# Moving the attention values' products two score tiles behind their pair's second turn

## The chip, the cores and the metric

The kernel runs on one NeuronCore of a Trainium2 chip. The metric is the device time of one execution in microseconds (us). Two kernels are compared by runs on the same chip; the kernel before was run three times.

## What is computed

One layer of a hybrid encoder block on 512 tokens of width 2048, in float32: an adaLN-modulated RMS norm, one input projection, two token mixers that read the projected columns, a gate on each, one output projection, a gated residual and a last RMS norm. The part that matters here is the first mixer, attention with 16 heads of 64 columns. A query sees keys in three dilated windows; their outputs are merged with weights from the softmax denominators. Cut to its core, the reference says:

```python
for window, dilation in ((128, 1), (512, 4), (2048, 16)):
    o_p, lse_p = dilated_window_attention(aq, ak, av, rel_bias, window, dilation)
mix_w = jax.nn.softmax(jnp.stack(lses, axis=0), axis=0)
att = jnp.einsum('pbsh,pbshe->bshe', mix_w, jnp.stack(outs, axis=0))
```

The kernel folds the three patterns into one softmax: a key that several windows see gets the logarithm of its multiplicity, one that none sees gets a huge negative bias. So each head has one score matrix, one exponential, one normalisation and one product with the values.

## The kernel before

**Units.** TensorE is the engine whose order is written out by hand: `tc.manual_schedule(engines={E.PE})` makes its program order the order of the code. On the other engines (ScalarE, here ACT; VectorE, here DVE; GpSimd, here POOL; and SP, which issues most DMAs) the framework orders the instructions by priority and by what is ready. The large products are cut into units; `unit(name, ...)` computes 512 columns of the input projection in four PSUM chains. A unit has 8 groups of weights (two tiles of 128 input rows each), and in a group every chain gets two calls of `three` (L227 to L230): a product in high and low halves, three matmuls of 512 columns. Each call is a **tick**, so a unit has 64 ticks. The units `qk2`, `qk4`, `qk6` and `gk` follow one another, and each carries the attention of four heads as side work: a list of pairs (share of the unit, function). A function is called, and its TensorE instructions are thus placed, after the first tick that is not below its share times 64. What has a share of 1 or more goes into `spill` and comes at the head of the next unit.

**The attention items.** `attention(pairs)` cuts four heads into 16 score tiles (4 per head, `h`, `i`), numbered here 0 to 15, and has three kinds of items for them.

- `score(h, i)`, L819 and L820: two matmuls (128 queries, 416 keys) into a PSUM tile `s`; DVE adds the bias and takes the extreme (L827, two pieces), ACT takes the exponential with its sum (L831), DVE the reciprocal (L834), POOL scales the tile `p` (L842; for the last two tiles of head 15 ACT does, L840). An odd tile is scaled in two pieces, one of which goes into free columns of the even tile's buffer. The second tile of a head also issues the DMA of the next head's bias (L806, on SP's queue).
- `turn(h, i)`, L857: three transposes of `p` into a PSUM tile `t`; ACT copies its high half (L861) and DVE subtracts for the low half (L862), both into the buffer `pt`. The turn of an odd tile calls `rest` (L870): a fourth transpose, into a tile `r` of the PSUM ring `pj`, of the columns that the pair shares, then two small copies on ACT (L875) and two small subtractions on DVE (L877).
- `values(h, e)`, L886: for a pair of tiles eight matmuls of 256 columns into a PSUM tile `o`, over four chunks of keys and the high and low halves of `pt`, chunk 0 last; ACT copies half of the result (L889) and DVE adds it to the other half (L893).

`pt` exists twice, one for each pair of a head, and the next head writes the same two again. `s`, `t` and `o` share the PSUM ring `pa` with three buffers, so each of these items takes the buffer of the third one before it. The ring `pj` has five: four for the unit's chains and one for `r`.

**Their order.** The list of items is built by a loop over `x`: score tile `x`, then the turn of tile `x - 2`, then, where that tile is odd, the values of the pair that ends with tile `x - 3`. The 40 items are spread evenly over the unit, from share 0.17 on, 0.02 apart; the first two are moved a little ahead, and the last one, the values of pair 14/15, is moved behind the unit's end, to the first tick of the next.

**Around it.** While the heads of one unit are worked on, the unit computes the queries and keys of later heads. After its last tick `qk_evict` (L757 on) moves them out of PSUM: for each head two ACT copies (L766, L773) and two DVE operations (L767, L775), with DMAs to make the other half's copies. The chains of the next unit need these PSUM buffers. After `gk` four ACT copies (L1265) do it. Beside the scores DVE also splits weights (L476, behind ACT's L492) and does sums that other stages need.

Of the kernel before, what the change touches and what calls it, by code (L numbers as in the profile page):

```python
# [189 lines left out]
def block_kernel(ctx: ExitStack, tc: tile.TileContext, a: dict):  # L190
# [485 lines left out]
    n = len(chain) // 2  # L676
# [121 lines left out]
    def attention(pairs):  # L798
# [47 lines left out]
        def turn(h, i):  # L846
            def go():
                e, half = divmod(i, 2)
                if len(pts) == e:
                    pts.append(B8(f"pt{e}", [2, 4, 256], F32R))  # L850
                    nc.gpsimd.memset(pts[e][:, :, 3, 0:P].bitcast(F32), 0.0)
                    nc.gpsimd.memset(pts[e][:, :, 0, P:2 * P].bitcast(F32), 0.0)
                pt, t = pts[e], pr_[h, i]
                pk = PA(f"t{h}{i}")
                first_ = 0 if half else 128
                for kt in range(3):
                    nc.tensor.transpose(pk[:, kt * P:kt * P + P], t[:, first_ + kt * P:first_ + kt * P + P], ident)  # L857
                hi = pt[:, 0, half:half + 3, P * half:P * half + P]
                lo = pt[:, 1, half:half + 3, P * half:P * half + P]
                src = pk[:, :3 * P].rearrange("p (k q) -> p k q", k=3)  # L860
                act(hi, src, AF.Copy)  # L861
                tt(lo, src, hi.bitcast(F32), op=ALU.subtract)  # L862
                if half:
                    rest(h, e)
            return go
# [13 lines left out]
        def values(h, e):  # L879
            def go():  # L880
                t = pts[e]
                po = PA(f"o{h}{e}")
                order = (1, 2, 3, 0)
                for n_, c in enumerate(order):
                    for w in range(2):
                        mm(po[:, :256], vv[h // 4][:, CHUNK_OF[e][c], h % 4, :], t[:, w, c, :],  # L886
                           start=n_ == 0 and w == 0, stop=n_ == 3 and w == 1)
                oh = sm.tile([64, 256], F32, tag="oh", name=f"oh{h}{e}", bufs=1)
                act(oh, po[64:128, :256], AF.Copy)  # L889
                own = stacks[h][3]  # L890
                p = h // 2
                dst = cat[p // 4][own, p % 4, :].rearrange("p (c e) -> p e c", e=2)[:, 1 - e, :]
                tt(dst[:, ::-1], po[0:64, :256], oh, op=ALU.add)  # L893
            return go

        items = []
        n = len(tiles)
        for x in range(n + 3):
            if x < n:
                items.append(score(*tiles[x]))  # L900
            if 2 <= x <= n + 1:
                items.append(turn(*tiles[x - 2]))
            v = x - 3
            if 0 <= v < n and tiles[v][1] % 2 == 1:
                items.append(values(tiles[v][0], tiles[v][1] // 2))
        g_load(heads[0])
# [348 lines left out]
    for n, p in (("qk2", 0), ("qk4", 2), ("qk6", 4)):  # L1255
        ps = unit(n, False, attention((p, p + 1)) + ([(0.05, shift_row)] if p == 2 else []))
        for q in range(2):
            qk_evict(p + 2 + q, ps[2 * q], ps[2 * q + 1])

    ps = unit("gk", False, attention((6, 7)))  # L1260
    kp_.close()
    gs = mid.enter_context(tc.tile_pool(name="gs", bufs=1, reuse_waits="tile"))
# [237 lines left out]
    def keep(name, ps):  # L1500
        r = []
        for n, p_ in enumerate(ps):
            t = op.tile([P, 512], F32, tag="keep", bufs=7, name=f"{name}{n}")
            act(t, p_, AF.Copy)
            r.append(t)
        return r
# [148 lines left out]
    for pair, (l, r) in enumerate(OUT_PAIRS):  # L1655
# [17 lines left out]
        v = keep(f"v{pair}", g1)  # L1673
# [100 lines left out]
```

## Time and profile before

| what | us |
|---|---|
| median of three runs | 917.45 (916.46 to 918.5) |
| the profiled execution's own time | 918.13 |
| its span, first to last instruction | 916.3 |
| TensorE matmuls busy | 898.8 (98% of the span) |
| VectorE busy | 728.6 (80%) |
| ScalarE busy | 494.8 (54%) |
| GpSimd busy | 116.4 (13%) |
| mean granted TensorE clock | 0.996 of full |

How to read it. A row of a timeline has the start and the duration in us, the engine, the line, the operation, the tiles written and read, the shape and a count of merged instructions; in brackets stands the idle time of the engine before it and what ended the idle time. Matmuls are pipelined: one of 256 columns is shown with about 0.28 us although the next one starts much sooner, so the time that a stretch of TensorE costs is read from the start of its first matmul to the start of the one behind it. A view of waits sums who waited for whom; a view of windows gives each engine's busy time in a stretch of the span, the granted clock and the share of the DMA engines that is in use.

### The profile page before, as it was taken

To read this page: it belongs to the slowest core of one execution; us is meant where nothing else is said; L and a number is where in the kernel's file an instruction comes from. 1 tells how busy PE (TensorE), PEld (TensorE's weight loads), DVE (VectorE), ACT (ScalarE), POOL (GpSimd) and SP (SyncE) were. 2 spreads that over 40 slices of the span, in tenths; PEclk is the share of its full clock that TensorE was granted. 3 is DMA by queue.
4 is the path that set the end of the run, shared out by engine and by line. 5 is a ranking of instruction groups with operands and counts; after the bars stand their busy time and mean duration, and the time that the engine had idled before them with its cause. 6 is when DMAs were issued, how large, how long until landed. Compare 5 with 4: busy or idle time off the path is not lost.

```text
span 916.3 us, 12554 instructions
## 1 busy us (share of the span) xinstructions
PE 898.8 (98%) x4295; PEld 747.8 (82%) x4295; DVE 728.6 (80%) x1235; ACT 494.8 (54%) x855; POOL 116.4 (13%) x203
## 2 busy tenths in 40 slices
PE   8999999999999999999999999999999999999996
PEld 6888888888888888888778788888888888888874
DVE  7988799878779888888659668585786559798687
ACT  5563533566655655655647564273654338455454
POOL 0000000022323223223100111111120100000001
PEclk9999999999999999999999999999999999999999
DMA  9999498587799898897878868877787887878763
GB/s 344 403 412 394 175 364 306 173 255 205 210 268 275 246 266 247 242 278 223 251 241 257 299 204 272 256 221 232 214 286 223 259 265 276 289 285 261 284 221 154
DMA packets 64202, 241.30 MB, mean 263 GB/s; under 512 B 8357, under 2 KB 10693, under 8 KB 54537
## 3 DMA queue, kind: packets, MB, share of 16 engines
q1 hardware_dynamic: 57378, 198.18, 61.1%
q0 software_dynamic: 6464, 42.01, 19.3%
q8 instruction: 34, 0.56, 0.3%
q10 hardware_dynamic: 296, 0.30, 0.1%
q14 instruction: 30, 0.25, 0.1%
HBM read 224.64 MB, written 51.47 MB: 301 GB/s over the span
## 4 chain that ended last, share of the span: by engine, by line
PE 87%; DVE 5%; ACT 3%; DMA 2%; issue 1%; POOL 0%; DVEq 0%; ACTq 0%
PE ps_qk L228 4%; PE ps_qk L230 4%; PE ps_qk L229 4%; PE g L230 4%; PE g L228 4%; PE g L229 4%; PE stb L230 3%; PE stb L228 3%; PE stb L229 3%; PE ps_ag L230 3%; PE ps_ag L228 3%; PE ps_ag L229 3%; PE o L886 3%; PE sta L229 3%; PE sta L230 3%; PE sta L228 3%
## 5 line engine op out<-in xcount | busy, mean ns | idle before, releaser
L327 DVE CUSTOM_DVE_ANT_0 cb<-cb,sb,c_bcond 128x2048 f32<-128x2048 f32 (+1 forms) x32 | 73.4, 2295 | 0.9 <-DMA cb<-in_wm 0.9
L842 POOL TENSOR_SCALAR p<-p,st 128x416 f32<-128x416 f32 (+2 forms) x93 | 49.8, 541 | 179.8 <-DVE st L834 97.0
L831 ACT ACTIVATE p<-p,st 128x416 f32<-128x416 f32 x64 | 41.1, 642 | 46.8 <-DVE st L827 40.2
L428 POOL DMA_DIRECT2D T<-in_w_o x32 | 23.1, 723 | 166.0 <-ACT V2h L492 14.0
L886 PEld LDWEIGHTS o<-pt,vv 128*128 128x128 f32 x256 | 35.3, 188 | 9.1 <-DVE pt L877 4.6
L886 PE MATMUL o<-pt,vv 128*128 128x256 f32 x256 | 38.8, 286 | 3.6 <-DVE pt L877 2.9
L862 DVE TENSOR_TENSOR pt<-t,pt 128x384 fp32r<-128x384 f32 x64 | 35.4, 553 | 7.0 <-ACT pt L861 6.2
L861 ACT ACTIVATE pt<-t 128x384 fp32r<-128x384 f32 x64 | 31.5, 492 | 17.5 <-PE t L857 16.4
L827 DVE CUSTOM_DVE_ANT_0 p<-s,g 128x160 f32<-128x160 f32 x64 | 23.6, 369 | 19.9 <-PE s L820 18.7
L857 PEld LDWEIGHTS t<-c_ident,p 128*128 128x128 f32 x192 | 24.9, 140 | 8.4
L857 PE MATMUL t<-c_ident,p 128*128 128x128 f32 x192 | 31.3, 272 | 0.0
L827 DVE CUSTOM_DVE_ANT_0 p<-s,g,st 128x256 f32<-128x256 f32 x64 | 27.4, 428 | 1.3
L1057 ACT ACTIVATE sq<-st,sc 128x256 f32<-128x256 f32 x24 | 12.2, 507 | 19.3 <-DVE st L1047 11.3
L819 PE MATMUL s<-ks,qh 128*128 128x416 f32 x64 | 22.5, 351 | 0.0
L820 PE MATMUL s<-ks,ql 128*128 128x416 f32 x64 | 22.5, 351 | 0.0
L327 DVE CUSTOM_DVE_ANT_0 rawg<-rawg,crow,c_bcond 128x1024 f32<-128x1024 f32 x16 | 20.3, 1279 | 2.3 <-DMA rawg<-in_wg 2.3
L1547 POOL TENSOR_SCALAR x<-x,rn 128x512 f32<-128x512 f32 x2 | 2.3, 1170 | 149.6 <-ACT rn L1536 145.2
L327 DVE CUSTOM_DVE_ANT_0 rawg<-rawg,crow,gate 128x1024 f32<-128x1024 f32 x16 | 20.4, 1280 | 1.1 <-DMA rawg<-in_wg 1.1
L428 POOL DMA_DIRECT2D T3V<-in_w_gv x8 | 5.5, 693 | 119.8 <-ACT qk21h L492 119.8
L465 DVE TENSOR_TENSOR raw_O<-raw_O,raw_P 128x1024 f32<-128x1024 f32 x8 | 9.8, 1226 | 12.2 <-DMA raw_O<-in_w_o 8.3
L889 ACT ACTIVATE oh<-o 64x256 f32<-64x256 f32 x32 | 12.2, 382 | 12.8 <-PE o L886 12.0
L877 DVE TENSOR_TENSOR pt<-r,pt 32x128 fp32r<-32x128 f32 x64 | 17.9, 280 | 1.0
(1660 smaller groups left out, 3127.4 us busy)
## 6 DMA issues: line engine op xcount, KB each, us to landing
cb<-in_wm SPq DMA_DIRECT2D x31, 1024.0 KB, 9.2
T<-in_w_o POOLq DMA_DIRECT2D x32, 512.0 KB, 5.7
rawg<-in_wg SPq DMA_DIRECT2D x32, 512.0 KB, 5.6
raw_O<-in_w_o SPq DMA_DIRECT2D x32, 512.0 KB, 4.5
raw_qk<-in_w_qk SPq DMA_DIRECT2D x24, 512.0 KB, 4.6
raw_O<-T SPq DMA_DIRECT2D x24, 512.0 KB, 4.9
rawb<-in_w_sb SPq DMA_DIRECT2D x16, 512.0 KB, 5.5
rawv<-in_wv SPq DMA_DIRECT2D x16, 512.0 KB, 4.6
```

The lines of the kernel that those rows point to most:

```text
L228: mm(ps, lh, rh, start=first, stop=False, skip_group_check=more)
L229: mm(ps, ll, rh, start=False, stop=False, skip_group_check=more)
L230: mm(ps, lh, rl, start=False, stop=last, skip_group_check=more)
L327: return nc.vector.tensor_tensor_reduce(out=w, in0=w, in1=with_, op0=ALU.mult, op1=ALU.add, scale=1.0, scalar=init, accum_out=dst)
L428: move = nc.gpsimd.dma_start(dst, src, max_dma_last_dim=8192, **how).ins
L827: top = nc.vector.tensor_tensor_reduce(out=t[:, lo:hi], in0=ps[:, lo:hi], in1=gt[h][:, at:at + 2 * (hi - lo) - 1:2], op0=ALU.add, op1=ALU.min,
L831: act(t, t, AF.Exp, bias=st[:, 0:1], scale=-1.0, accum_out=st[:, 1:2])
L842: last["pool"] = nc.gpsimd.tensor_scalar(to, of, st[:, 2:3], 1.0, op0=ALU.mult, op1=ALU.mult).ins
L857: nc.tensor.transpose(pk[:, kt * P:kt * P + P], t[:, first_ + kt * P:first_ + kt * P + P], ident)
L861: act(hi, src, AF.Copy)
L862: tt(lo, src, hi.bitcast(F32), op=ALU.subtract)
L886: mm(po[:, :256], vv[h // 4][:, CHUNK_OF[e][c], h % 4, :], t[:, w, c, :], start=n_ == 0 and w == 0, stop=n_ == 3 and w == 1)
```

## The change

Two numbers in the loop that builds the list of items:

```diff
         items = []
         n = len(tiles)
-        for x in range(n + 3):
+        for x in range(n + 4):
             if x < n:
                 items.append(score(*tiles[x]))
             if 2 <= x <= n + 1:
                 items.append(turn(*tiles[x - 2]))
-            v = x - 3
+            v = x - 4
             if 0 <= v < n and tiles[v][1] % 2 == 1:
                 items.append(values(tiles[v][0], tiles[v][1] // 2))
```

The list still has 40 items, and their shares are the same. Within it the values of a pair go two places back, and the odd score tile and the odd turn that stood behind them go one place forward. Before, the order around a pair was: second turn, score, turn, values. After, it is: second turn, score, turn, score, turn, values of the pair; directly ahead of them stands the second turn of the next pair. At the end of a unit, `turn 14, values 13, turn 15 | values 15` becomes `turn 14, turn 15, values 13 | values 15`, where the bar is the unit's end.

With `s`, `t` and `v` for score, turn and values, and the tile's number (for `v` that of the pair's odd tile), the ticks after which the items stand, worked out from the list and the shares:

| item | before | after |
|---|---|---|
| even scores and turns, s0 to s3, t0 to t2 | the same | the same |
| s5, s7, s9, s11, s13, s15 | 24, 30, 36, 43, 49, 56 | 22, 29, 35, 41, 48, 54 |
| t3, t5, t7, t9, t11, t13, t15 | 25, 31, 38, 44, 50, 57, 61 | 24, 30, 36, 43, 49, 56, 59 |
| v1, v3, v5, v7, v9, v11, v13 | 22, 29, 35, 41, 48, 54, 59 | 25, 31, 38, 44, 50, 57, 61 |
| v15, in the next unit | 65 | 65 |

The ticks from a pair's second turn to its values thus go from 4 (pairs 1, 3, 5, 9, 11, 15), 3 (pair 7) and 2 (pair 13) to 7 or 8 (pairs 1 to 11), 5 (pair 13) and 6 (pair 15).

## The prediction

> **What bounds the kernel now.** First the page: its part 1, and of part 5 the group of the moved matmuls.
>
> ```profile
> PE 898.8 (98%) x4295; PEld 747.8 (82%) x4295; DVE 728.6 (80%) x1235; ACT 494.8 (54%) x855; POOL 116.4 (13%) x203
> ...
> L886 PE MATMUL o<-pt,vv 128*128 128x256 f32 x256 | 38.8, 286 | 3.6 <-DVE pt L877 2.9
> ```
>
> TensorE is busy for 98% of the span, so the end moves with what TensorE has to do and with what it waits for. The change leaves its work as it is: 4295 matmuls, in another order. What can change is its waiting. The second row shows that the moved group, 256 matmuls of L886, has 3.6 us of idle time ahead of its members, most of it ended by the last small subtraction of `rest` (L877).
>
> Second, the view of windows, over the four attention units: from the first matmul of `qk2` to the values of pair 15 in the last of them.
>
> ```profile
> 188.00:453.00 265.00, 261.43 (x1385) 221.98 (x1385) 220.87 (x617) 158.89 (x361) 72.89 (x132) 1.00 0.86 251
> ```
>
> After the stretch and its length stand the busy times of PE, weight loads, DVE, ACT and POOL, then the granted clock (full) and the DMA share. 265.00 - 261.43 = 3.57 us: all the idle time that TensorE has in these units is that of L886. Nothing else in them makes it wait: no score, no transpose, no weight, no DMA. DVE is at 83%, ACT at 60%, POOL at 28%, and the DMA engines at 0.86.
>
> Third, the view of waits, for PE:
>
> ```profile
> PE o L886 <- DVE pt L877: 2.9, 5, 0.9
> ```
>
> Five waits, and they are for data, the last piece of `pt`. Fourth, the timeline of TensorE at these places. First a values group that does not wait, then the first and the last of those that do.
>
> ```profile
> 220.66 1.12 PE L886 MATMUL o<-pt,vv 128*128 128x256 f32 x8
> 221.62 0.40 PE L228 MATMUL ps_qk<-h_hi,qk24h 128*128 128x512 f32 x1
> ...
> 246.81 1.03 PE L886 MATMUL o<-pt,vv 128*128 128x256 f32 x5
> ...
> 248.34 0.62 PE L886 MATMUL o<-pt,vv 128*128 128x256 f32 x3 [0.50 <-DVE pt L877]
> 248.80 0.40 PE L228 MATMUL ps_qk<-h_hi,qk27h 128*128 128x512 f32 x1
> ...
> 444.49 0.93 PE L886 MATMUL o<-pt,vv 128*128 128x256 f32 x4
> ...
> 447.01 0.39 PE L228 MATMUL ps_gk<-h_hi,gk7h 128*128 128x512 f32 x1
> ```
>
> From its first start to the start of the projection matmul behind it an undisturbed group takes 221.62 - 220.66 = 0.96 us. The group at 246.81 takes 1.99 and the one at 444.49 takes 2.52. Of the 32 groups seven are long. In order of time they take 1.99, 1.34, 2.01, 2.16, 1.99, 1.35 and 2.52 us, 13.36 together, against 7 x 0.96 = 6.72. So the waits cost TensorE **6.64 us**. That is more than the 3.57 us of idle time, because a matmul's shown end lies behind the point at which the next could have started, and because the matmul after a wait starts a new pipeline.
>
> Which seven they are says why. By the ticks at which they stand, four are the values of pair 13 (one in each unit, together 8.51 - 3.84 = 4.67 us), which stand two ticks behind their pair's second turn; one is pair 7 of `qk6` (three ticks, 1.20 us); two are pair 9 of `qk4` and `gk` (four ticks, 0.77 us). It is distance that lacks.
>
> **The change part by part.**
>
> *What it adds and removes:* no instruction, no DMA, no buffer. PE executes 32 groups of 0.96 us as before.
>
> *The values move back.* What must lie between a second turn and its values is the chain transposes, ACT copies, DVE subtractions. Here it is for pair 13 of `qk2`, and its slowest case, pair 7 of `qk6`:
>
> ```profile
> 244.65 0.49 PE L857 MATMUL t<-c_ident,p 128*128 128x128 f32 x3
> ...
> 245.97 0.49 ACT L861 ACTIVATE pt<-t 128x384 fp32r<-128x384 f32 x1
> ...
> 248.00 0.29 DVE L877 TENSOR_TENSOR pt<-r,pt 32x128 fp32r<-32x128 f32 x1
> ...
> 249.50 0.40 PE L228 MATMUL ps_qk<-h_hi,qk27h 128*128 128x512 f32 x1
> ```
>
> ```profile
> 354.97 0.49 PE L857 MATMUL t<-c_ident,p 128*128 128x128 f32 x3
> ...
> 359.56 0.29 DVE L877 TENSOR_TENSOR pt<-r,pt 32x128 fp32r<-32x128 f32 x1
> ```
>
> The chain needs 248.29 - 244.65 = 3.64 us in the first and 359.85 - 354.97 = 4.88 us in the second. A tick is 249.50 - 248.80 = 0.70 us. After the change pair 13 has five ticks and the values of pair 11 between: 5 x 0.70 + 0.96 = 4.46 us, without the two turns that also lie there. That covers 3.64. The other pairs have seven or eight ticks, 4.9 us at least, and two scores and two turns on top; that covers even 4.88. So all seven waits should go: **-6.6 us**. Counting by the idle rows alone it would be -3.6; I take the starts, since they are what the stream loses, and keep 3.6 as the small end.
>
> *The odd scores and turns move forward* by one place. A score and its own turn keep their distance in ticks, except for tiles 3 and 7, which lose one. The shortest case is tile 3, whose turn also loses the values of pair 1 ahead of it:
>
> ```profile
> 271.60 0.85 POOL L842 TENSOR_SCALAR p<-p,st 128x384 f32<-128x384 f32 x2 [1.05 <-PE t L857]
> ...
> 275.42 0.49 PE L857 MATMUL t<-c_ident,p 128*128 128x128 f32 x3
> ```
>
> The scaled tile is ready at 272.45, the turn comes at 275.42: 2.97 us of cover, less 0.70 and 0.96, leaves 1.3. Cost: nothing. The bias DMA of the next head is issued with an odd score and comes at most two ticks earlier on SP's queue; its buffer has been free since two scores before, as now. The POOL scaling of the odd tiles moves past POOL's own DMA issues; POOL is busy for 28% of these units. Both cost nothing as long as that holds; if POOL were late by more than 1.3 us, the turns would wait.
>
> *The PSUM ring.* Each item still takes the buffer of the third one before it, but they are other pairs now: an odd score takes that of an earlier pair's values. The nearest is score 11, three ticks behind the values of pair 5. These are the slowest such values that were themselves not held up:
>
> ```profile
> 351.57 1.12 PE L886 MATMUL o<-pt,vv 128*128 128x256 f32 x8
> ...
> 354.72 0.42 DVE L893 TENSOR_TENSOR cat<-o,oh 64x256 f32<-64x256 f32 x1
> ```
>
> Their buffer is free 355.14 - 351.57 = 3.57 us after they begin. Between them and score 11 lie 3 x 0.70 + 0.96 = 3.06 us, a score and an even turn. The score is short:
>
> ```profile
> 208.98 0.35 PE L819 MATMUL s<-ks,qh 128*128 128x416 f32 x1
> ...
> 209.36 0.39 PE L228 MATMUL ps_qk<-h_hi,qk23h 128*128 128x512 f32 x1
> ```
>
> With its 0.38 us that is 3.44 us and the turn's transposes. So this place is tight: nothing to some tenths of a microsecond, in four units. I take nothing and keep 0.5 in the range. The others have four ticks, 3.76 + 0.38 = 4.1 us and more.
>
> *The unit's end.* Without the wait of pair 13 TensorE reaches the next unit about a microsecond earlier, while DVE is still emptying the old chains:
>
> ```profile
> 321.78 0.69 DVE L767 TENSOR_TENSOR ks<-ps_qk,ks 64x512 fp32r<-64x512 f32 x1
> ...
> 323.54 0.39 PE L228 MATMUL ps_qk<-h_hi,qk60h 128*128 128x512 f32 x1
> ```
>
> The last `ks` subtraction ends at 322.47, and the first matmul of the next unit's fourth chain, which needs a buffer that was freed by then, starts at 323.54. That leaves 1.07 us against the 1.05 us that pair 13 gives up here (2.01 - 0.96). DVE itself idled behind that wait and moves forward too, so I take nothing and keep one microsecond at each of the three such ends for the range.
>
> *A rule that speaks against it.* The view of waits names L877, which fills `pt`. The Trainium skill, "Perfetto Trace Analysis", section "Optimization Strategy", says that a bubble that repeats on the engine that should be saturated can mean that there is not enough SBUF or PSUM for the next tile. By it the bubble at the values would be the ring's three buffers, which the change does not add to, and the sum would be zero. The trace speaks against that here: L877 reads `r` of the other ring and releases no buffer of this one.
>
> *The sum:* -6.6 us. The profiled execution took 918.13 us with a span of 916.3, so such an execution would take 911.5; from the median of 917.45 it gives **910.8 us**.
>
> **The rivals.**
>
> *Part of it is given back.* The chains' buffers at three unit ends take up to 1.0 us each, or score 11's buffer up to 0.5 in four units. For it: 1.07 us of cover against 1.05. Against it: DVE has idle time there which it also wins. With the three ends in full it would be 910.8 + 3.0 = 913.8 us; counting the gain by the idle rows alone gives 917.45 - 3.6 = 913.9, the same place.
>
> *The waits come again.* The ends of the `pt` pieces are set by the order that the framework gives to DVE, not by the turn; if DVE's order puts L877 later now that its reader is later, TensorE waits as before. The time stays at 917.4. It ends the same way if the bubble is one of buffers: then the group waits for the ring wherever it stands, and the chance below covers both. That is the reading of the Trainium skill's page named above. Against it: with two ticks all four groups are long, with three one of four, with four ticks two of 24; lateness follows the distance.
>
> *Slower: the ring of three.* In each unit six items take a values buffer, five of them odd scores. If ACT and DVE give that buffer back late, each of the six waits. The latest row of the trace is that of the group at 444.49:
>
> ```profile
> 449.45 0.42 DVE L893 TENSOR_TENSOR cat<-o,oh 64x256 f32<-64x256 f32 x1
> ```
>
> 449.87 - 444.49 = 5.38 us. If all took so long, the five with four ticks would wait for about 1.0 us (5.38 - 4.4, with score, turn and ticks between) and score 11 for 1.7: 6.7 per unit, 26.8 in all, less 6.6 is +20.2 or 937.7 us. It decides against the change when the 24 items wait for more than 0.28 us on average, that is from a release of about 4.6 us on. Against it: 1.56 us of the 5.38 are that group's own wait, which goes; the slowest undisturbed group has 3.57.
>
> **How the numbers follow.** Chances: the forecast, all seven waits gone and at most a microsecond and a half given back, 0.74 (909.6 to 912.3, with the spread of the three runs, 1 us each way); part given back, 0.13 (912.3 to 915.6); the waits come again, 0.07; slower, 0.06. The range 909.6 to 914.5 holds nearly all of the first and most of the second, about 0.82, and leaves the last two out. A measurement of this kernel tells about 0.2%, 1.8 us, from no change: faster than 915.6 holds the first two cases, 0.87; within 0.2%, 0.07; slower, 0.06.
>
> **What would show it.** In the changed kernel's profile the group L886 should have no idle time, the waits of PE should have no row with L877, and all 32 groups should take 0.96 us. The four units should span 258.4 us instead of 265.0, with TensorE busy throughout. It is wrong if PE shows new waits: a score that waits for DVE's L893 (the ring), the first projection matmuls of a unit waiting for L767 or L775 (the chains), or a turn that waits for POOL's L842. If the units are 6.6 us shorter and the end is not, a later stage has taken it back; the windows of the stages behind 453 us would show where.

## The result and the profile after

| what | before | after |
|---|---|---|
| median of six runs each on one chip, us | 917.31 (916.46 to 920.28) | 912.57 (911.63 to 913.05) |
| ratio of the two, with its 95% interval | | 0.9942 (0.9932 to 0.9952) |
| the profiled execution's own time | 918.13 | 913.05 |
| its span | 916.3 | 911.2 |
| mean granted TensorE clock | 0.996 | 0.996 |

The change makes the kernel 4.7 us faster. The forecast was 6.6 us: the sign is right, and the kernel is 1.8 us slower than forecast (912.57 us against 910.8). That lies in the stated range, but in the part of it that belonged to the rival "Part of it is given back" (912.3 to 915.6, chance 0.13) and not in that of the forecast (up to 912.3, chance 0.74). Of the kernel after, first part 1 of the page and, of its part 5, the group of the moved matmuls.

```profile
PE 896.0 (98%) x4295; PEld 746.6 (82%) x4295; DVE 726.9 (80%) x1235; ACT 492.9 (54%) x855; POOL 114.1 (13%) x203
...
L886 PE MATMUL o<-pt,vv 128*128 128x256 f32 x256 | 35.4, 281 | 0.0
```

The idle time ahead of L886 was 3.6 us and is 0.0; the group's own busy time falls from 38.8 to 35.4 us as well. The 32 groups, read from their first start to the start of the matmul behind them, take 30.22 us together and 0.95 at most; before they took 37.14. Next the waits of PE, the whole list that the view gives.

```profile
PE sta L585 <- ACT h_hi L531: 1.5, 1, 1.5
PE warm L294 <- DVE hot L306: 1.5, 1, 1.5
PE s L819 <- DMA ks<-ks: 1.1, 1, 1.1
PE sta L229 <- DVE h_lo L534: 0.8, 1, 0.8
PE sta L228 <- ACT h_hi L531: 0.7, 1, 0.7
PE kv L1040 <- DVE gv L1388: 0.5, 1, 0.5
```

No row names L877 any more, and none names L893 (the ring), L842 (GpSimd's scaling), L767 or L775 (the chains' buffers). But a row is new: a score waits for the DMA that copies keys, L770. It is one wait, in the timeline of `qk6`'s head; first the kernel before at the same place, then the kernel after.

```profile
317.29 0.51 SPq L770 DMA_DIRECT2D ks<-ks  x1
...
325.57 0.35 PE L819 MATMUL s<-ks,qh 128*128 128x416 f32 x1
326.65 0.35 PE L819 MATMUL s<-ks,qh 128*128 128x416 f32 x1
```

```profile
315.54 0.55 SPq L770 DMA_DIRECT2D ks<-ks  x1
...
323.81 0.35 PE L819 MATMUL s<-ks,qh 128*128 128x416 f32 x1
...
326.11 0.43 PE L819 MATMUL s<-ks,qh 128*128 128x416 f32 x1 [1.06 <-DMA ks<-ks]
```

These are score tiles 0 and 1 of the unit. Tile 1 is the first to read the key columns that L770 copies (its 416 columns begin at 256, the copied ones at 512). Before, the two tiles stand 1.08 us apart, after 2.30 us: the wait costs 1.22 us by starts. Tile 1 had 0.8 us to spare before: the trace has the copy landing at 325.86 and the score at 326.65. After, `qk4` ends earlier and the copy is issued earlier, at 315.54 and not at 317.29. Yet it lands at 325.97. From issue to landing it takes 10.43 us where it took 8.56.

Set unit by unit, from the first score of one unit to that of the next (for `gk` to the matmul behind its last values), what was taken away and what arrived:

| stretch | before | after | gain | waits of the values taken away | given back |
|---|---|---|---|---|---|
| `qk2` | 65.34 | 64.56 | 0.78 | 1.04 | 0.26 |
| `qk4` | 65.59 | 64.15 | 1.44 | 1.47 | 0.03 |
| `qk6` | 66.37 | 65.46 | 0.91 | 2.24 | 1.33 |
| `gk` | 60.61 | 59.00 | 1.61 | 1.97 | 0.36 |
| all four | 257.91 | 253.17 | 4.74 | 6.72 | 1.98 |

The fifth column is what the seven long groups took above 0.95 us. So the whole forecast gain is there, and 2.0 us are lost again, 1.22 of them at that one score; at the heads of `qk2` and `gk` score tile 1 stands about 0.25 us further behind tile 0 than before. The one of `qk2` lies ahead of everything that the change moves, and in the other traces that leave tile 1 at its tick it stands there between 1.07 and 1.54 us behind tile 0; so that part is spread of the executions, and about 1.7 us are left as the price of the change. The two spans differ by 916.32 - 911.25 = 5.07 us. The 0.33 us that lie outside these stretches are 0.46 us more for the start-up in this execution and 0.79 us less for the stages behind the attention.

### The profile page after: what moved, and what is told of

It reads as the page before. It is cut to its first block, busy times and chain, and to the rows that moved or that the text cites. A ratio compares the mean times of both kernels' runs of the same rounds, so it can differ in the third digit from the quotient of the medians.

```text
span 911.2 us, 12579 instructions
## 1 busy us (share of the span) xinstructions
PE 896.0 (98%) x4295; PEld 746.6 (82%) x4295; DVE 726.9 (80%) x1235; ACT 492.9 (54%) x855; POOL 114.1 (13%) x203
## 4 chain that ended last, share of the span: by engine, by line
PE 88%; DVE 4%; DMA 4%; ACT 2%; issue 1%; SPq 0%; DVEq 0%; ACTq 0%
PE ps_qk L228 4%; PE ps_qk L229 4%; PE ps_qk L230 4%; PE g L230 4%; PE g L229 4%; PE g L228 4%; PE stb L230 3%; PE stb L229 3%; PE stb L228 3%; PE ps_ag L230 3%; PE ps_ag L228 3%; PE ps_ag L229 3%; PE o L886 3%; PE sta L229 3%; PE sta L230 3%; PE sta L228 2%
## 5 line engine op out<-in xcount | busy, mean ns | idle before, releaser
L842 POOL TENSOR_SCALAR p<-p,st 128x416 f32<-128x416 f32 (+2 forms) x93 | 47.6, 520 | 177.3 <-DVE st L834 134.5
L428 POOL DMA_DIRECT2D T<-in_w_o x32 | 23.1, 722 | 167.8 <-ACT V2h L492 15.1
L886 PEld LDWEIGHTS o<-pt,vv 128*128 128x128 f32 x256 | 34.7, 189 | 2.9
L886 PE MATMUL o<-pt,vv 128*128 128x256 f32 x256 | 35.4, 281 | 0.0
L428 POOL DMA_DIRECT2D T3V<-in_w_gv x8 | 5.6, 697 | 119.8 <-ACT qk21h L492 119.8
L877 DVE TENSOR_TENSOR pt<-r,pt 32x128 fp32r<-32x128 f32 x64 | 17.8, 278 | 1.0 <-ACT pt L875 0.6
L562 ACT ACTIVATE h_hi<-xt,shift 128x512 fp32r<-128x512 f32 x16 | 11.5, 719 | 12.9 <-DVE shift L327 12.9
```

Of the source, the lines that this page charges most:

```text
L428: move = nc.gpsimd.dma_start(dst, src, max_dma_last_dim=8192, **how).ins
L842: last["pool"] = nc.gpsimd.tensor_scalar(to, of, st[:, 2:3], 1.0, op0=ALU.mult, op1=ALU.mult).ins
```

## The experiments

Theory: the values waited for distance, and with distance all seven waits go; the heads of the units then run into the copies of queries and keys, whose landing is set by the DMA engines being full and not by the time of issue. Rivals: distance is not what mattered, but a buffer; the head's wait is one of SP's queue, or an accident of one execution. All ratios are against runs of the kernel before on the same chip. In all of these kernels the whole computation is done.

**The kernel after once more, and score tile 1 later.** The second moves score tile 1 away from its copy, by a smaller fourth number in the attention's shares (tick 12); a variant puts it at tick 11.

```diff
-ATT_AT = (0.17, 0.8, 0.04, 0.05, 0.05)
+ATT_AT = (0.17, 0.8, 0.04, 0.02, 0.05)
```

> The changed kernel as it is, as the measure for the other runs of this call. Copies theory: the seven waits at the values (6.6 us) stay gone, and about 1.9 us come back as waits of score tiles 0 and 1 at the heads of the units, above all in qk6, because the DMA that copies a head's keys lands no earlier than before (at 325.97 us, before 325.86) while TensorE is there 1.7 us sooner: 4.7 us faster than before (ratio 0.995), with a wait of PE s on a DMA of ks of 1 us or more. Chance theory: the wait at 326 us belongs to that one execution; in a second profile it is gone and the attention units are 6.6 us shorter.

> The changed kernel with score tile 1 of each unit two ticks later (share 0.18, tick 12 instead of 10), nothing else. Copies theory: tile 1 is the first to read the copied key columns; two ticks are 1.4 us of projection work in front of it, so its wait of 1.2 us in qk6 and the small one in gk go, and the kernel gets 1.0 to 1.5 us faster than the changed one (911.3, ratio to before 0.9935). Rival, the waits have another cause (DVE emptying the old chains, or the score's own PSUM buffer): moving tile 1 alone changes nothing, or its turn at tick 18, now six ticks behind, waits for POOL: same as the changed kernel or slower by up to 1 us.

> The changed kernel with score tile 1 one tick later instead of two (tick 11). Copies theory: 0.7 us of projection work in front of it takes 0.5 to 0.7 us off its wait in qk6, and turn 1 keeps 1 us of cover, so that r does not wait for POOL: 0.3 to 0.7 us faster than the changed kernel, ratio 0.9935 to 0.9942. If the transfers are so irregular that the wait only moves to another copy (qh or ql, tile 0), the time stays that of the changed kernel.

The kernel after took 911.85 us (ratio 0.9944, 0.9928 to 0.9961), and its one wait of note in the attention came again:

```profile
PE s L819 <- DMA ks<-ks: 0.5, 1, 0.5
```

So it is no accident, though its size varies: 0.5 us where 1 us or more had been expected. The copy is issued at 314.62 in this trace and lands at 324.50. Tile 1 at tick 12 took 912.57 us (0.9942, 0.9922 to 0.9962), at tick 11 911.5 (0.9936, 0.9923 to 0.995, 0.035 in place of 0.02). Of tick 12 the waits of PE:

```profile
PE r L870 <- POOL p L842: 0.5, 1, 0.5
PE s L819 <- DMA qh<-qh: 0.5, 1, 0.5
PE s L819 <- DMA ks<-ks: 0.2, 1, 0.2
```

The wait for keys goes down to 0.2 us, but turn 1 now comes too close behind tile 1 for GpSimd's scaling, and the first score of `qk2`, ahead of the moved tile, waits for its queries. The expected gain of more than a microsecond did not come: a miss, though an interval of almost 4 us could not show it by the time alone; the rival that named GpSimd was half right. Tick 11 has the same waits of `r` (not expected there) and of 0.2 us for keys, and cannot be told from the kernel after.

**Only pair 13, and all but pair 13.** Two kernels exchange the last turn and the values of pair 13 in the list of items; one does it to the kernel before (values of pair 13 behind turn 15, everything else as before), the other to the kernel after (values of pair 13 back ahead of turn 15).

```diff
+        items[37], items[38] = items[38], items[37]
```

> The kernel before with one exchange: the values of pair 13 stand behind turn 15 instead of ahead of it (tick 61 instead of 59); all other values stay one score tile behind. Distance theory: the four long groups of pair 13 go (4.67 us), pairs 7 and 9 keep theirs (2.0 us), and since the units' ends come earlier as in the changed kernel, the same 1 to 2 us come back at the next units' heads: 2.5 to 4.5 us faster than before (ratio 0.995 to 0.997). Rival, the order on DVE sets the waits and not the distance: pair 13 still waits, ratio 1.000.

> The changed kernel with one exchange: the values of pair 13 stand ahead of turn 15 again (tick 59, turn 15 at 61), three ticks behind their turn and with the values of pair 11 between; all else as changed. Distance theory: three ticks, one values group and a turn are about 3.4 us, the chain needs 3.5 to 3.8 us there, so pair 13 waits for 0 to 0.4 us in each unit, pairs 7 and 9 not at all; 4 to 5 us faster than before, within 1 us of the changed kernel (ratio 0.9945 to 0.9960). That would say that the gain at the unit's end comes from moving score 15 and turn 13 forward and not from the place of pair 13 itself. Rival, only the place behind turn 15 helps: pair 13 waits for about 1 us in each unit as before, ratio 0.9985 to 1.000.

The first took 919.62 us, slower than before (1.0025, 1.0013 to 1.0037), where 2.5 to 4.5 us of gain had been expected. Its waits of PE in the attention:

```profile
PE r L870 <- DVE pt L877: 2.4, 3, 0.8
PE r L870 <- ACT gkt L1266: 1.5, 1, 1.5
...
PE o L886 <- DVE pt L877: 0.9, 1, 0.9
```

The values of pair 13 wait no longer, but the transpose `r` of turn 15 does. It now stands two ticks behind that of turn 13 (before: four), and the ring `pj` has one buffer for `r`: it must wait until L877 has read the one before (in `gk`, the second row, by the profile for an ACT copy of the unit's chains, L1266). In the changed kernel turn 13 has moved forward too, three ticks lie between the two, and no `r` waits. So moving the values alone is not the gain; the turns had to move with them. That is a term that the prediction did not have.

The second took 914.18 us (0.9961, 0.9946 to 0.9975), 3.6 us faster than before where 4 to 5 had been expected. Its longest wait of PE in the attention:

```profile
PE o L886 <- DVE pt L862: 0.5, 1, 0.5
```

Here pair 13 waits in no unit, although its values stand only three ticks behind its second turn (before: two); the values of pair 11 lie between. So the earlier turn 13 is already enough, and the last exchange of the change is not needed for pair 13. It is needed for the last pair: with turn 15 later, the values of pair 15 wait in `gk` in this trace (the row shown).

**Only the unit's end.** The kernel before with the changed order for the last items alone: pairs 1 to 9 stay where they were.

```diff
+        items[33:36] = items[34], items[35], items[33]
+        items[37], items[38] = items[38], items[37]
```

> The kernel before, with the order of the changed one at the end of each unit alone (score 15, turn 13, values 11, turn 14, turn 15, values 13); up to there the values stay one score tile behind. Distance theory: the four waits of pair 13 go (4.7 us) and turn 15 finds its buffer, since score 15 and turn 13 came forward too; pairs 7 and 9 keep their waits (2.0 us); about 1.5 us come back at the next units' heads. 2.5 to 4 us faster than before (ratio 0.9955 to 0.9975), no wait of r on L877 as in the run that moved pair 13 alone. Rival, the whole order has to change for the end to gain: r or t wait at the end as in that run, ratio 1.000 or above.

It took 917.1 us (0.999, 0.9978 to 1.0002): no gain that can be told from none, where 2.5 to 4 us had been expected. Its waits of PE in the attention, and its timeline at the longest:

```profile
PE s L819 <- DMA ks<-ks: 2.8, 2, 1.5
...
PE o L886 <- DVE cat L893: 1.8, 1, 1.8
PE o L886 <- DVE pt L877: 1.1, 2, 0.9
```

```profile
441.70 1.11 PE L886 MATMUL o<-pt,vv 128*128 128x256 f32 x8
...
446.32 0.63 ACT L1274 ACTIVATE lrs<-lrb 128x512 fp32r<-128x512 f32 x1 [3.51 <-DMA lrb<-in_w_lr]
446.98 0.38 ACT L889 ACTIVATE oh<-o 64x256 f32<-64x256 f32 x1
...
447.71 0.42 DVE L893 TENSOR_TENSOR cat<-o,oh 64x256 f32<-64x256 f32 x1
448.18 1.22 PE L886 MATMUL o<-pt,vv 128*128 128x256 f32 x8 [1.81 <-DVE cat L893]
```

Three things at once. The waits of pair 13 are gone and those of pairs 7 and 9 are still there (1.1 us of idle time, L877): each wait answers to its own pair's distance, which is what the theory says. The heads lose 2.8 us to the copies of keys, where about 1.5 had been expected. And in `gk` the rival of the ring appears in one place: the buffer of pair 11's values, begun at 441.70, is given back at 448.13, 6.4 us later, because ACT takes its half of the result only at 446.98: it stands idle for 3.51 us until a load has landed (L1274), which its order has ahead of that copy. The changed kernel takes the same buffer for the same item and has no such wait, so this rival is real as a mechanism and decided nothing there.

**The copies by another queue.** The copies of keys are issued from ACT's queue, so that nothing on SP's queue is ahead of them.

```diff
-                nc.sync.dma_start(both[..., 512:768].bitcast(F32), both[..., 0:256].bitcast(F32))
+                nc.scalar.dma_start(both[..., 512:768].bitcast(F32), both[..., 0:256].bitcast(F32))
```

> The changed kernel with the copies of the keys issued from ACT instead of SP; order of everything else unchanged. Copies theory, if they are late because they stand behind weight loads of SP's queue: the wait of tile 1 in qk6 goes and the kernel gets about 1 us faster than the changed one, landing in 2 to 5 us instead of 9 to 10. If they are late because all 16 DMA engines are taken: they still land 8 us or more after the issue and the time stays within 0.5 us. ACT pays about 0.4 us of issue each, 12 in all, beside TensorE.

It took 916.69 us (0.9993, 0.9984 to 1.0003), 4.8 us more than the kernel after on the same chip, where a difference of at most 0.5 us had been expected. The waits of PE, and one row of ACT:

```profile
PE t L857 <- POOL p L842: 1.4, 2, 0.9
...
PE r L870 <- POOL p L842: 1.1, 1, 1.1
PE s L819 <- DMA qh<-qh: 1.1, 1, 1.1
...
PE s L819 <- DMA ks<-ks: 0.4, 1, 0.4
```

```profile
327.21 1.06 ACT L492 ACTIVATE qk63h<-raw_qk 128x1024 fp32r<-128x1024 f32 x1 [6.05 <-DMA qh<-qh]
```

The copy of that head, issued at 316.49, lands at 326.16, 9.7 us later and at nearly the same time as by SP's queue. So SP's queue is not what holds it. The loss is at other places, at the turns, which wait for scaled tiles. ACT's order now has such an issue (at 326.48) ahead of the split of weights in the row shown; ACT stands idle for 6.05 us ahead of that split, which comes at 327.21 and in the kernel after at 323.33. That this is what makes the scaled tiles late is argued and not shown.

**The other transfers earlier or later.** The DMA engines are full at the units' ends. Here the window of the kernel after around `qk6`'s head (the last two columns are the share of the DMA engines and GB/s):

```profile
311.00:326.00 15.00, 14.05 (x74) 11.67 (x71) 11.41 (x23) 8.96 (x17) 2.74 (x5) 1.00 0.96 251
```

Among them are large transfers from POOL's queue for sums of weight blocks that a later stage needs (`paced`, L428, 512 KB each), spread evenly over the four units by `block_sums` (L457). Issued at 311.6 to 312.7, they land at 320.8 to 325.0. Their shares of the unit were changed: all of them by 0.75; by 0.25 + 0.75 of the share; by 0.75 in `qk4` and `qk6` only; and, in the last two kernels, by 0.75 in `qk4` and `qk6` and in `qk2` only from share 0.15 on, alone and with score tile 1 at tick 11.

```diff
-        return [((q + 0.5) / n, x) for q, x in enumerate(r)]
+        lo, f = {"qk2": (0.15, 0.7), "qk4": (0.0, 0.75), "qk6": (0.0, 0.75)}.get(name, (0.0, 1.0))
+        at = [(q + 0.5) / n for q in range(n)]
+        return [(min(a, lo) + f * max(a - lo, 0.0), x) for a, x in zip(at, r)]
```

> The changed kernel with the DMA steps of the block sums (POOL's queue) pressed into the first three quarters of each unit; the same steps, the same order. Copies theory, DMA engines taken: fewer bulk transfers stand ahead of the copies at the unit's end, the keys of qk6's first head land 2 us or more sooner after their issue (6 to 8 us instead of 9.9 to 10.4), the wait of score tile 1 in qk6 goes, and the kernel is 0.5 to 1.3 us faster than the changed one (ratio 0.993). Rival, the copies are late for another reason (SP's queue, their own small packets): the wait stays, the same time as the changed kernel.

> The opposite: the block sums' DMA steps pressed into the last three quarters of each unit. Copies theory: more bulk transfers stand ahead of the copies, which land 1 to 3 us later; score tile 1 waits for 2 us or more in qk6 and also in gk or qk4, and the kernel is 1 to 4 us slower than the changed one (ratio 0.996 to 0.999). Rival: no difference.

> The changed kernel with the block sums' DMA steps pressed into the first three quarters of the units qk4 and qk6 alone, so that the head of qk2 and everything behind gk are left as they are. Copies theory: the copies for the heads of qk6 and gk land sooner, as they did when all units were pressed (7.5 us after the issue), the waits of score tiles 0 and 1 there go (0.7 to 1.3 us), and nothing is lost at the head of qk2: ratio 0.9930 to 0.9940, 0.5 to 1.3 us faster than the changed kernel. Rival: the sums' transfers then collide with something else, the same time as the changed kernel or slower.

> The changed kernel with the block sums' transfers moved ahead in three units, and the start of the first kept: in qk2 the sums from share 0.15 on at 0.7 of their distance from it, in qk4 and qk6 all at 0.75 of their share. Theory (the 1.9 us given back are copies of keys that land late because the sums' transfers fill the DMA engines at the end of a unit): no score waits at the heads of qk4, qk6 and gk (earlier sums removed those waits), and the head of qk2 stays as in the changed kernel (0.1 to 0.3 us), because the first two sums of qk2 are where they were. About 910.5 to 911.5, 1 to 2 us below the changed kernel. Rival (whatever is taken off one place of the DMA engines comes back at another): a wait of 0.5 to 1.7 us at some head or at a turn, and 912 to 913.

> As the kernel with the sums' transfers moved ahead in three units, and in addition score tile 1 two ticks later than the first planned, at tick 11. Theory: with the copies landing in time the later tile adds nothing at the heads; its turn then comes closer behind it and can wait for GpSimd's scaling (0.5 us once, as it did in the run with tile 1 at tick 11 alone). About 911, the same as the kernel beside it within 0.7 us. Rival (heads still short of copies): 0.5 to 1 us faster than the kernel beside it.

| kernel | us | ratio (95%) |
|---|---|---|
| all earlier | 917.91 | 1.0002 (0.9991 to 1.0013) |
| all later | 912.24 | 0.9945 (0.9929 to 0.9961) |
| earlier in `qk4`, `qk6` | 912.71 | 0.9943 (0.9931 to 0.9955) |
| earlier in three units, start of `qk2` kept | 910.6 (909.88 to 912.08) | 0.9917 (0.9903 to 0.9931) |
| the same with tile 1 at tick 11 | 911.17 | 0.9917 (0.9903 to 0.9931) |

All earlier: at the heads of `qk4`, `qk6` and `gk` no score waits at all, as expected. But the total is that of the kernel before, where a little less than that of the kernel after had been expected. Two of the waits of PE behind the attention, the first sums of `qk2` on POOL, and a window behind the first score:

```profile
PE kv L1040 <- DVE gv L1388: 1.4, 1, 1.4
...
PE z L988 <- DVE lrst L1301: 0.9, 1, 0.9
```

```profile
184.80 1.01 POOL L428 DMA_DIRECT2D T3V<-in_w_gv  x2 [119.77 <-ACT qk21h L492]
```

```profile
198.00:204.00 6.00, 6.00 (x21) 4.94 (x21) 3.08 (x10) 1.47 (x4) 2.52 (x4) 0.72 1.18 294
```

Two sums of `qk2` now go out together ahead of the copies for its own head, where the kernel after sends one; a score waits 1.67 us, and behind it the granted clock falls to 0.72 over six microseconds. Yet the larger part of the loss is elsewhere. Against the trace of the kernel after, the first score comes 1.5 us later, the four stretches take the same (253.3 and 253.2 us), and the part behind them takes 3.1 us more, where the rows of L1040 and L988 show longer waits; why, stays open.

All later: 0.6 us of the wait for keys remains, and the loss of 1 to 4 us that had been expected did not come. The transfers at the end of `qk4` stand at about the same time as in the kernel after, so this run tells little there. The head of `qk2` tells more: its copy of keys that is issued between 190.9 and 191.8 lands after 2.3 us with no sum just ahead of it (all later), after 3.9 and 4.4 us with one (the kernels before and after; 3.9 to 5.7 us over the eleven traces with one that issue it on SP's queue), and after 6.0 us with two (all earlier).

Earlier in two units: no wait at the heads of `qk6` and `gk`, but one at that of `qk4`, and no gain over the kernel after, where 0.5 to 1.3 us had been expected. Ahead of that head the last two sums of `qk2`, which had not been moved, and the first two of `qk4`, which now stand ahead of its first score, go out together, four between 246.2 and 247.8, where the kernel after has three (line numbers of this kernel are one higher):

```profile
PE s L820 <- DMA ks<-ks: 1.1, 1, 1.1
```

That led to the version that moves the sums of three units and leaves the first ones of `qk2` in place (lines two higher). The head of `qk6` in it, and the window around that:

```profile
323.67 0.35 PE L821 MATMUL s<-ks,qh 128*128 128x416 f32 x1
...
324.75 0.35 PE L821 MATMUL s<-ks,qh 128*128 128x416 f32 x1
```

```profile
311.00:326.00 15.00, 15.00 (x78) 12.83 (x77) 11.41 (x22) 8.80 (x17) 1.76 (x4) 1.00 0.93 230
```

No score waits for keys; tiles 0 and 1 stand 1.08 us apart again; TensorE is busy in the whole of the window. Part 6 of the profile's page (count, KB each, median us from issue to landing) has the copies of keys, before, after, and here:

```profile
ks<-ks SPq DMA_DIRECT2D x8, 128.0 KB, 7.6
```

```profile
ks<-ks SPq DMA_DIRECT2D x8, 128.0 KB, 9.0
```

```profile
ks<-ks SPq DMA_DIRECT2D x8, 128.0 KB, 6.6
```

The four stretches of the table take 64.71, 64.15, 64.23 and 58.70 us, 251.79 in all: 6.12 us less than before, against 4.74 for the change alone (5.4 in its second trace). One wait is left in the attention, 0.7 us for queries at the very first score, ahead of these stretches. At 910.6 us this has the lowest median of the study. Its interval ends just below that of the first timing of the kernel after (0.9931 against 0.9932) and overlaps that of the second (0.9928 to 0.9961), and the two were not timed side by side; so by the times alone the further gain of 1 to 2 us is likely and not certain. With tile 1 at tick 11 on top it is no faster, as expected when the copies are in time.

## Why the prediction came out as it did

**The values move back: right.** Seven waits were to go, 6.6 us by starts; all seven went, 6.7. Counting by starts and not by the 3.57 us of idle rows was the right choice: the small end of 3.6 is well below what the units won, even net of the loss. That distance was the reason is shown by the run of the unit's end, where the pairs that kept their distance kept their waits, and by the one in which pair 13 at three ticks does not wait. The rival "The waits come again" is out, and with it the rule of the Trainium skill's page "Perfetto Trace Analysis", section "Optimization Strategy", for this place: the waits went (0.0 us of idle time ahead of L886) with the ring's three buffers as before.

**The odd scores and turns move forward: not free.** No turn waits for L842, as forecast, and without this move the exchange at the unit's end only moves the wait to `r`. But "Cost: nothing" rested on POOL being idle enough, and what it overlooked are the transfers that POOL issues. `paced` issues a sum's transfer behind the scaling that stands ahead of it in the code. At the end of `qk4` the sum at share 0.85 stood ahead of score 15 (share 0.86) and now stands behind it (0.84). POOL at this place, before and after:

```profile
308.53 0.80 POOL L428 DMA_DIRECT2D T2V<-in_w_gv  x1
312.26 0.85 POOL L842 TENSOR_SCALAR p<-p,st 128x384 f32<-128x384 f32 x2 [2.92 <-DVE st L834]
313.06 0.54 POOL L428 DMA_DIRECT2D T4V<-T2V  x1
313.59 0.82 POOL L428 DMA_DIRECT2D T4V<-in_w_gv  x1
```

```profile
310.82 0.85 POOL L842 TENSOR_SCALAR p<-p,st 128x384 f32<-128x384 f32 x2 [3.09 <-DVE st L834]
311.61 0.79 POOL L428 DMA_DIRECT2D T2V<-in_w_gv  x1
312.13 0.80 POOL L428 DMA_DIRECT2D T4V<-T2V  x1
312.65 1.09 POOL L428 DMA_DIRECT2D T4V<-in_w_gv  x1
```

Where two transfers of 512 KB left together, three do, and the copies of keys come behind them. All seven traces with score 15 in its new place and the sums where they were have three, and the copy takes 9.7 to 10.9 us; the kernel before and the one that exchanges pair 13 alone have two, and it takes 8.6. Of the five kernels with moved sums all have two; in four the copy takes 7.5 to 8.4 us, but in "all later" 10.1, which does not fit. No run moves this one transfer alone, so it is likely and not shown that it makes the copies late.

**The PSUM ring: right.** No score waits for L893 in the kernel after; by its trace the tightest odd score behind a values' buffer has 0.9 us to spare, and the tightest item of the ring, a turn, 0.38 us. A release as late as the rival needs (4.6 us and more) occurs once in the kernel after (5.3 us) and delays nothing there; where one decides (6.4 us, in the run of the unit's end) it does so once.

**The unit's end: the step that failed.** "I take nothing" should have been a loss of about 2 us, so the sum of -6.6 us promised that much too much. The prediction looked for the next thing late at this end in the PSUM chains, L767 and L775, and found 1.07 us of cover, which held. The late thing was one step further: L767 is followed by the DMA L770, and that by score tile 1 of the next unit. The sentence that nothing else made TensorE wait, "no DMA", was true of the kernel before and said nothing of how near the next wait was: 0.8 us, as two points of its trace show. The rival "Part of it is given back" had the place and, at the lower edge of its interval, the time (912.3 to 915.6 us), and the wrong resource. That the copies land late because of the other transfers at the units' ends is shown by the runs that move only those transfers: in the four that send them earlier in `qk4` and `qk6` no score waits for keys at the heads behind, and at `qk2`'s head the way of the copy grows with the number of sums just ahead of it. That it is not SP's queue is shown by the copies on ACT's queue. That the landing stays put to 0.1 us while the issue moves by 1.75 us is chance, since in the second trace of the kernel after it is 1.4 us earlier; what all traces of this order with the sums in their places show is the longer way, 9.9 to 10.9 us against 8.6. Its likely cause are the three sums that now leave together.

## What to carry to other kernels

When a stall on the saturated engine is to go, list for each place that then comes earlier not only what waits today but what is nearly late, with its slack, through DMAs to their landing. Look as well at which transfers are issued behind the moved items: they move too, and can bunch. A transfer among full DMA engines need not land earlier when it is issued earlier; here the issue came 1.75 us sooner and the way was 1.9 us longer. And an order of three kinds of items is moved as a whole or tested as one: two of the three partial versions here were no faster than the kernel before. One shifted the wait to the buffer of `r`; the other lost its gain to the copies of keys and to a values' buffer that came back late.

## What was not expected of the hardware

A wait can cost more than its idle time. In the kernel with all sums earlier, TensorE stood idle for 1.67 us ahead of a score, and some 1.2 us later its matmuls slowed down:

```profile
196.64 0.42 PE L819 MATMUL s<-ks,qh 128*128 128x416 f32 x1 [1.67 <-DMA qh<-qh]
...
199.29 0.63 PE L229 MATMUL ps_qk<-h_hi,qk21l 128*128 128x512 f32 x1
199.72 0.63 PE L230 MATMUL ps_qk<-h_lo,qk21h 128*128 128x512 f32 x1
...
202.32 0.40 PE L229 MATMUL ps_qk<-h_hi,qk21l 128*128 128x512 f32 x1
202.56 0.39 PE L230 MATMUL ps_qk<-h_lo,qk21h 128*128 128x512 f32 x1
```

For about 3.4 us the starts lie 0.43 us apart and not 0.24, at a granted clock of 0.72 in that window: an estimate from these starts is 1.5 us lost beyond the wait (some 3.4 us at little more than half the pace). The 1.81 us wait in the run of the unit's end had no such effect; the window 448 to 454 us there has the full clock. The same shows at the start-up: behind waits of 2.40 us (the kernel before) and 2.30 us (the second trace of the kernel after) the clock from 11.5 to 14.5 us is 0.50, behind waits of 2.29 and 2.19 us at the same place (the last kernel of the table; all but pair 13) it is 1.00. What tells the cases apart stays open.
